# The first of eight feed-forward blocks computed with seven half-sized products, and 320 bytes less of small tiles

## The chip, the cores and the metric

The kernel runs on one core of a Trainium2 chip, in one launch. The metric is device time in microseconds (us): the median over runs of the same program on the chip. TensorE (PE) does the matmuls, VectorE (DVE) and ScalarE (ACT) the elementwise work, GpSimd (POOL) and SyncE (SP) here mostly issue DMAs.

## The reference

One layer of a diffusion backbone for 512 tokens of 2048 features, all in fp32: differential attention and a convolution module, an output projection, a layer norm, and a feed-forward part (FFN) of 8192 inner features with a second layer norm. What the change touches is the end:

```
x  = layer_norm(alpha * x + g1 * y, ln1_g, ln1_b)
h2 = layer_norm(x) * (1 + sc2) + sh2
x  = layer_norm(alpha * x + g2 * (square(relu(h2 @ w_ff1 + b_ff1)) @ w_ff2 + b_ff2), ln2_g, ln2_b)
```

`g2`, `sc2` and `sh2` come from the conditioning vector.

## The kernel before

**Products.** Every fp32 product is three matmuls (`mm3`, L118 to L121): each operand is split into a high part, a rounded copy made by ScalarE (L105), and a low part, the difference made by VectorE (L106). In the names `wh` and `wl` are the halves of a weight tile `w` of 128 x 1024, `h2h` and `h2l` those of the normed input, `fh` and `fl` those of the squared relu. Each weight tile is loaded on SP's queue, copied on ScalarE and subtracted on VectorE before TensorE can use it. `turn["w"]` is the list of pools that the split weights take their tiles from in turn.

**The FFN** goes in eight blocks of 1024 inner features, q = 0 to 7. A block first makes the inner features, eight products n of 128 features with two weight tiles each (tile `f`), then multiplies them with its part of `w_ff2`. There are two ways for the second product:

- `down` (tile `d`): 4 column groups c, 4 pairs of inner features j; 384 matmuls of 512 columns, and the result is multiplied by `g2` and added to the residual `res` at once (`add_gated`). Blocks 0 and 7 use it.
- `down_s` (tile `p`): the 2 x 2 block product of a column half with seven instead of eight half-sized products, 336 matmuls. It needs sums and differences of the inner features (`u1`, `u2`, made on VectorE from a pair of features, tiles `ft` and `fz`) and of weight tiles (L1177). Its sums go to DRAM tensors `accd` on POOL's queue, accumulating from the second block on. Blocks 1 to 6 use it; `ahead` prepares the weights four steps early.

**Block 0** is done in two halves of 256 tokens, because the first layer norm is still running on the second half: `side` is a list of generators whose steps (the projection's end, `ln1_a`, `ln1_b`) are put between the products. The first half goes n = 0 to 7, the second 7, 0 to 6 with the weights of n = 7 kept. Then `gate2` loads `g2`, and `down(0, c, ...)` runs with `bias2` between its weight tiles: eight times a row of `b_ff2` is loaded, multiplied by `g2` (L1091) and added to the residual (L1092). Half of each residual is stored to the DRAM tensors `x1d` on SP's queue after every second c. Block 7 reads `x1d` and `accd` back in `restore` (L1277 to L1279) under its `hidden`, adds its own product, and does the second layer norm.

The order within an engine's queue is not the program's: a scheduler reorders what the functions issue, by its own estimates, before the program is built.

**Where tiles lie.** In each partition the pools lie one behind the other. `const`, `upool` (function `unit`), `rpool`, `wpool` and `tpool` come first, then `small`. `small` begins at a multiple of 512 bytes (185,344) and each of its tiles takes a multiple of 32 bytes. It holds 2880 bytes, which is 5 x 512 + 320, so every pool opened after it, `xw` and `st` among them, begins 320 bytes past a multiple of 512 (188,224), and their large tiles with it. `Pair` gives the weights of blocks 1 to 6 in turn with `wpool`: its `wh` is a tile of `st`, its `wl` one of `upool`.

```
    class Pair:
        def tile(self, shape, dt, tag=None, name=None):
            return unit(name, shape, dt) if tag == "wl" else st.tile(list(shape), dt, tag="H", name=name, bufs=2)

    turn["w"] = [wpool, Pair()]
```

Of the kernel before, what the change touches and what calls it, by code (L numbers as in the profile page):

```python
# [63 lines left out]
def dit_block(ctx, tc, A, out):  # L64
# [1021 lines left out]

    def bias2():
        for i in range(2):
            for t in range(4):
                b = row(5, i, f"bf{t}_{i}")  # L1090
                V.tensor_tensor(b, b, g2[i], op=ALU.mult)  # L1091
                V.tensor_tensor(res[t][i], res[t][i], b, op=ALU.add)  # L1092
                yield

    hid = [None] * 4
# [41 lines left out]
    def hidden_s(n):  # L1137
# [13 lines left out]
        if n % 2:  # L1151
            i = n % 8 // 2
            z = tmp(f"fz{n}", (P, 4, 256))
            V.tensor_tensor(z[:, 0], t[:, 3], t[:, 1], op=ALU.subtract)
            V.tensor_tensor(t[:, 1], t[:, 0], t[:, 1], op=ALU.subtract)
            V.scalar_tensor_tensor(z[:, 1], z[:, 0], -1.0, t[:, 0], op0=ALU.mult, op1=ALU.subtract)
            V.scalar_tensor_tensor(z[:, 2], z[:, 1], -1.0, t[:, 2], op0=ALU.mult, op1=ALU.subtract)
            split(u1[i][0], u1[i][1], t)
            split(u2[0][:, i], u2[1][:, i], z[:, 0:3])
# [284 lines left out]
```

## Time and profile before

| | |
|---|---|
| median of 3 runs | 2401.72 us (2399.5 to 2401.82) |
| profiled execution, its own time | 2405.81 us |
| its span on the core | 2404.0 us |
| mean granted TensorE clock | 0.995 |
| TensorE busy | 2346.1 us, 98% |
| VectorE busy | 1614.9 us, 67% |
| ScalarE busy | 884.0 us, 37% |
| POOL busy | 129.1 us, 5% |

The profiled execution is 4.1 us above the median, and its span is 1.8 us shorter than its time. Times in the trace count from the start of the span. A matmul's row shows a duration that overlaps with the next ones, so the pace is read from the starts. The stages of the FFN, by the first matmul of each: block 0's first half from 1016.65, its second half from 1077.00, `down(0)` from 1124.83, block 1 from 1216.08, block 7 from 2216.01, its `down` from 2304.05.

### The profile page before, as it was taken

How to read it: one execution, taken by the hardware profiler on the slowest of the kernel's cores; microseconds unless marked ns; L12 is line 12 of the kernel's file. 1: busy time of each engine (PE TensorE's matmuls, PEld its weight loads, DVE VectorE, ACT ScalarE, POOL GpSimd, SP SyncE). 2: the span in 40 equal slices, each digit the busy share in tenths (PEclk: the TensorE clock that was granted, in tenths of full speed). 3: DMA queues.
4: the chain of work that ended last, by engine and by line, in shares of the span. 5: the costliest groups of instructions: out<-in, count | busy, mean ns of one | idle time of the engine just before them, and what ended most of it. 6: DMA issues, size and time to landing. Idle time of an engine off the chain costs nothing.

```text
span 2404.0 us, 29326 instructions
## 1 busy us (share of the span) xinstructions
PE 2346.1 (98%) x11476; PEld 1866.2 (78%) x11476; DVE 1614.9 (67%) x2136; ACT 884.0 (37%) x1205; POOL 129.1 (5%) x196
## 2 busy tenths in 40 slices
PE   6999999999999999989999999999999999999998
PEld 4777767777677888889787888888888888888886
DVE  5656999942758777767536846747658558467577
ACT  5223411122535666464223333333334333333322
POOL 0000000000011210000000100100101101002000
PEclk9999999999999999999999999999999999999999
DMA  8665466876877645236542442743534615627652
GB/s 336 246 219 197 164 215 214 289 271 244 293 223 209 164 115 175 88 121 207 173 144 76 159 164 71 165 142 97 141 114 106 192 54 125 192 69 155 214 191 105
DMA packets 126298, 410.87 MB, mean 171 GB/s; under 512 B 15048, under 2 KB 21576, under 8 KB 126160
## 3 DMA queue, kind: packets, MB, share of 16 engines
q1 hardware_dynamic: 107728, 360.76, 43.7%
q0 software_dynamic: 18432, 48.25, 10.0%
q8 instruction: 90, 1.47, 0.3%
q14 instruction: 48, 0.39, 0.0%
HBM read 359.65 MB, written 49.30 MB: 170 GB/s over the span
## 4 chain that ended last, share of the span: by engine, by line
PE 89%; DVE 4%; DMA 3%; ACT 2%; issue 1%; SPq 0%; POOL 0%; DVEq 0%; ACTq 0%
PE f L119 9%; PE f L121 9%; PE f L120 9%; PE p L120 6%; PE p L119 6%; PE p L121 6%; PE gb L219 2%; PE u L119 2%; PE u L120 2%; PE u L121 2%; PE o L580 2%; PE v L119 2%; PE d L121 2%; PE d L120 2%; PE v L120 2%; PE v L121 2%
## 5 line engine op out<-in xcount | busy, mean ns | idle before, releaser
L106 DVE TENSOR_TENSOR wl<-w,wh 128x1024 fp32r<-128x1024 f32 x334 | 404.1, 1221 | 392.1 <-ACT wh L105 391.9
L105 ACT ACTIVATE wh<-w 128x1024 fp32r<-128x1024 f32 x334 | 351.3, 1059 | 742.4 <-PE f L120 274.0
L121 PE MATMUL f<-h2h,wl 128*128 128x512 f32 (+1 forms) x1152 | 425.9, 370 | 3.7 <-DVE wl L106 3.7
L119 PE MATMUL f<-h2h,wh 128*128 128x512 f32 (+1 forms) x1152 | 426.2, 370 | 0.1
L120 PE MATMUL f<-h2l,wh 128*128 128x512 f32 (+1 forms) x1152 | 423.3, 368 | 0.0
L121 PEld LDWEIGHTS f<-h2h,wl 128*128 128x128 f32 x1152 | 218.0, 189 | 44.5 <-DVE wl L106 5.4
L120 PEld LDWEIGHTS f<-h2l,wh 128*128 128x128 f32 x1152 | 218.0, 189 | 38.1
L119 PEld LDWEIGHTS f<-h2h,wh 128*128 128x128 f32 x1152 | 218.2, 190 | 37.2 <-ACT wh L105 0.3
L119 PE MATMUL p<-wh,u1h 128*128 128x512 f32 x384 | 151.5, 395 | 0.0
L120 PE MATMUL p<-wl,u1h 128*128 128x512 f32 x384 | 150.8, 393 | 0.0
L121 PE MATMUL p<-wh,u1l 128*128 128x512 f32 x384 | 149.9, 393 | 0.0
L342 DVE TENSOR_TENSOR ua<-ua,u 128x1024 f32<-128x1024 f32 x64 | 78.0, 1220 | 67.6 <-PE u L121 67.2
L1177 DVE TENSOR_TENSOR w<-w,w 128x1024 f32<-128x1024 f32 x96 | 115.9, 1218 | 0.8
L120 PE MATMUL p<-wl,u2h 128*128 128x512 f32 x288 | 113.7, 395 | 1.3 <-DVE wl L106 1.3
L121 PE MATMUL p<-wh,u2l 128*128 128x512 f32 x288 | 112.9, 392 | 0.0
L119 PE MATMUL p<-wh,u2h 128*128 128x512 f32 x288 | 112.8, 392 | 0.0
L119 PE MATMUL u<-hh,wh 128*128 128x512 f32 x256 | 102.7, 403 | 1.9 <-ACT hh L105 1.9
L120 PE MATMUL u<-hl,wh 128*128 128x512 f32 x256 | 101.9, 398 | 0.0
L121 PE MATMUL u<-hh,wl 128*128 128x512 f32 x256 | 101.1, 395 | 0.0
L282 DVE SCALAR_TENSOR_TENSOR cv<-cv,wdw 128x497 f32<-128x497 f32 (+14 forms) x120 | 89.0, 742 | 3.1
L119 PEld LDWEIGHTS p<-wh,u1h 128*128 128x128 f32 x384 | 72.0, 188 | 17.9 <-ACT u1h L105 1.5
L121 PEld LDWEIGHTS p<-wh,u1l 128*128 128x128 f32 x384 | 71.7, 188 | 17.4 <-DVE u1l L106 1.5
(301 smaller groups left out, 4460.3 us busy)
## 6 DMA issues: line engine op xcount, KB each, us to landing
w<-in_wff_dram SPq DMA_DIRECT2D x174, 512.0 KB, 5.0
wb<-in_wada_dram SPq DMA_DIRECT2D x128, 512.0 KB, 5.7
w<-in_wff2s_dram SPq DMA_DIRECT2D x96, 512.0 KB, 6.2
wa<-in_wada_dram SPq DMA_DIRECT2D x64, 512.0 KB, 6.1
wu<-in_wu_dram SPq DMA_DIRECT2D x32, 512.0 KB, 7.8
k<-kd POOLq DMA_DIRECT2D x64, 192.0 KB, 5.5
accd<-g POOLq DMA_DIRECT2D x48, 256.0 KB, 8.1
accd<-ev POOLq DMA_DIRECT2D x48, 256.0 KB, 5.4
```

The lines of the kernel that those rows point to most:

```text
L105: S.activation(hi, src, AF.Copy)
L106: V.tensor_tensor(lo, src, hi.bitcast(F32), op=ALU.subtract)
L119: T.matmul(ps, lhsT=ah, rhs=bh, start=first, stop=False)
L120: T.matmul(ps, lhsT=ah, rhs=bl, start=False, stop=False)
L121: T.matmul(ps, lhsT=al, rhs=bh, start=False, stop=last)
L219: T.matmul(gps[32 * g:32 * g + 32, 0:n], lhsT=cstat[:, kt, :], rhs=r[:, s * n:(s + 1) * n], start=kt < 4, stop=kt >= 12)
L282: V.scalar_tensor_tensor(dst[:, a:b], src[:, a + d:b + d], wdw[:, j, k:k + 1], dst[:, a:b], op0=ALU.mult, op1=ALU.add)
L342: V.tensor_tensor(uacc[j], uacc[j], ps, op=ALU.add)
L580: T.matmul(ops[:, qt * P:(qt + 1) * P], lhsT=es[1][:, kk * P:(kk + 1) * P], rhs=vh[:, kk, :], start=kk == 0, stop=kk == 5)
L1177: V.tensor_tensor(d, a, b, op=ALU.add)
```

## The change

Four things change together.

- Block 0 uses `down_s` too. A new `hidden_h` computes a product for one half of the tokens and writes the squared relu into one of four tiles `fts` that are kept over both halves; `combine`, the old body of `hidden_s`, runs on such a tile when both features of a pair have their second half. The second half of block 0's `hidden` now comes after the tiles of the first part are closed (`ff.close()`), with weights in `wpool` and `Pair` in turn. The layout of `w_ff2` gives `wff2s` seven blocks and `wff2` one.
- The residual is stored to `x1d` at the end of `ln1_a`, eight stores of 512 KB, on POOL's queue instead of SP's. Block 0's sums are the first to go to `accd`.
- `bias2` and the `gate2` ahead of it go. In block 7 `restore` loads two rows of `b_ff2`, multiplies them by `g2`, and adds them to the eight residual tiles: ten more VectorE operations of 128 x 1024.
- In `small` the filler grows from 8 to 24 floats, and the tiles `mv1`, `rs1`, `l2s`, `l2m` of four token groups and the four tiles `z` give way to four tiles of 16 floats. 64 bytes come, 640 go to 256: 2560 bytes are left, 5 x 512, and every later pool begins at a multiple of 512 bytes (187,904, which is 367 x 512).

```diff
-    small.tile([P, 8], F32, tag="fill", name="fill", bufs=1)
+    small.tile([P, 24], F32, tag="fill", name="fill", bufs=1)
...
-        def sm_(n, w):
-            return small.tile([P, w], F32, tag=f"{n}{g}", name=f"{n}{g}", bufs=1)
-
-        mv, rs, sm, mean = sm_("mv1", 2), sm_("rs1", 1), sm_("l2s", 4), sm_("l2m", 2)
+        sm_ = small.tile([P, 16], F32, tag=f"q{g}", name=f"q{g}", bufs=1)
+        mv, rs, sm, mean = sm_[:, 0:2], sm_[:, 2:3], sm_[:, 4:8], sm_[:, 8:10]
...
+        for i in range(2):
+            nc.gpsimd.dma_start(x1d[g][:, i * 1024:(i + 1) * 1024], us[i])
...
+    fts = [unit(f"ft0_{i}", (P, 4, 256)) for i in range(4)]
+
+    def hidden_h(n, half, keep=False):
+        ps = bk(f"f{n}_{half}")[:, 0:256]
+        sl = slice(256 * half, 256 * half + 256)
...
+        tv = fts[n // 2][:, 2 * (n % 2) + half, :]
+        S.activation(tv, ps, AF.Relu, bias=bff1[:, n:n + 1])
+        V.tensor_tensor(tv, tv, tv, op=ALU.mult)
...
-    turn["w"] = [wpool, xw, wpool]
-    for n in [7, *range(7)]:
-        hidden(n, (1,), hid)
-    turn["w"] = [wpool, wpool, xw]
-    gate2()
-    side.gs = [bias2()]
-    for c in range(4):
-        down(0, c, 0, 4, hid, 2)
-        if c % 2:
-            for t in range(4):
-                nc.sync.dma_start(x1d[t][:, (c // 2) * 1024:(c // 2) * 1024 + 1024], res[t][c // 2])
     ff.close()
...
+    def combine(i, t):
+        z = tmp(f"fz{i}", (P, 4, 256))
+        V.tensor_tensor(z[:, 0], t[:, 3], t[:, 1], op=ALU.subtract)
+        V.tensor_tensor(t[:, 1], t[:, 0], t[:, 1], op=ALU.subtract)
+        V.scalar_tensor_tensor(z[:, 1], z[:, 0], -1.0, t[:, 0], op0=ALU.mult, op1=ALU.subtract)
+        V.scalar_tensor_tensor(z[:, 2], z[:, 1], -1.0, t[:, 2], op0=ALU.mult, op1=ALU.subtract)
+        split(u1[i][0], u1[i][1], t)
+        split(u2[0][:, i], u2[1][:, i], z[:, 0:3])
...
-        if q == 1:
+        if q == 0:
             nc.gpsimd.dma_start(d, e)
...
-    for q in range(1, 7):
-        for n in range(8 * q, 8 * q + 8):
-            hidden_s(n)
...
+    for q in range(7):
+        if q == 0:
+            for m, n in enumerate([7, *range(7)]):
+                hidden_h(n, 1)
+                if n in (1, 3, 5, 6):
+                    combine(n // 2, fts[n // 2])
+                if m == 6:
+                    load_raw(q, 0, 1)
...
         load_raw(q, 0, 0)
+        if q == 0:
+            load_raw(q, 0, 2)
         load_raw(q, 0, 3)
...
     def restore():
+        b2 = [unit(f"b2_{i}") for i in range(2)]
         for i in range(2):
+            nc.sync.dma_start(b2[i], A["rows"][5:6, i * 1024:(i + 1) * 1024].partition_broadcast(P).rearrange("p a d -> p (a d)"))
+            V.tensor_tensor(b2[i], b2[i], g2[i], op=ALU.mult)
...
+                V.tensor_tensor(u, u, b2[i], op=ALU.add)
                 V.tensor_tensor(u, u, a, op=ALU.add)
...
-                sm = small.tile([P, 8], F32, tag=f"z{t}", name=f"zs{t}", bufs=1)
+                sm = small.tile([P, 16], F32, tag=f"q{t}", name=f"zs{t}", bufs=1)
```

The place that the prediction speaks of most is where block 0's second half of `hidden` ends and its second product begins. On VectorE before, the last weight splits `w_5_1`, `w_6_0` and `w_6_1` (inner product n, weight tile j) alternate with single squares, `fl` splits and the operations of `gate2` (L1084) and `bias2` (L1091, L1092):

```order
1104 L106 TENSOR_TENSOR wl<-w_5_1_9321,wh 128x1024
1105 L1084 TENSOR_TENSOR g_0_9422<-g_0_9422,bg_0_9424 128x1024
1106 L106 TENSOR_TENSOR wl<-w_6_0_9357,wh 128x1024
1107 L1056 TENSOR_TENSOR ft_9285<-ft_9285 128x256
...
1109 L106 TENSOR_TENSOR fl_8623<-ft_9285,fh_8622 128x256
1110 L106 TENSOR_TENSOR wl<-w_6_1_9387,wh 128x1024
1111 L1091 TENSOR_TENSOR bf_0_9442<-bf_0_9442,g_0_9422 128x1024
1112 L106 TENSOR_TENSOR wl<-w_0_0_0_9436,wh 128x1024
1113 L1056 TENSOR_TENSOR ft_9351<-ft_9351 128x256
1114 L1092 TENSOR_TENSOR r_0_5356<-r_0_5356,bf_0_9442 128x1024
```

After the change VectorE has here the chain of the third combine (`u1l_8884`, `u2l`), the split of `w_6_1`, two weight additions (L1173), and the chain of the fourth combine (tile `ft_3`). `w_0_0_0_0` and `w_0_0_0_1` are the weights of the second product's first steps:

```order
1111 L106 TENSOR_TENSOR u1l_8884<-ft_2_8264,u1h_8883 128x1024
1112 L106 TENSOR_TENSOR u2l<-fz_9336,u2h 128x768
1113 L106 TENSOR_TENSOR wl<-w_6_1_9380,wh 128x1024
1114 L1173 TENSOR_TENSOR w_0_0_0_0_9421<-w_0_0_0_0_9421,w_0_0_1_0_9345 128x1024
...
1116 L1099 TENSOR_TENSOR ft_3_8265<-ft_3_8265 128x256
1117 L1150 TENSOR_TENSOR fz_9412<-ft_3_8265 128x256
...
1121 L106 TENSOR_TENSOR u1l_8886<-ft_3_8265,u1h_8885 128x1024
1122 L106 TENSOR_TENSOR u2l<-fz_9412,u2h 128x768
1123 L106 TENSOR_TENSOR wl<-w_0_0_0_0_9421,wh 128x1024
1124 L106 TENSOR_TENSOR wl<-w_0_0_0_1_9423,wh 128x1024
```

What moved: the split of `w_6_1`, which stood behind a single `fl`, now stands behind a whole chain, and the splits of the first summed weights stand behind the next one.

On TensorE before, the last product of `hidden` (`f_1_9356`) ends whole and the second product (`d`) follows. After the change the last product (`f_1_9349`, n = 6) is cut: 26 of its matmuls stand ahead of 18 of the second product, that use the first three combines (u1h, u1l with the numbers 8879 to 8884), and 22 behind them:

```order
4765 L120 MATMUL f_1_9349<-h2l_8182,wh 128x256
4766 L119 MATMUL p_0_0_0_9451<-wh,u1h_8879 128x512
...
4783 L121 MATMUL p_0_0_1_9452<-wh,u1l_8884 128x512
4784 L121 MATMUL f_1_9349<-h2h_8181,wl 128x256
...
4805 L121 MATMUL f_1_9349<-h2h_8239,wl 128x256
4806 L119 MATMUL p_0_1_0_9470<-wh,u2h 128x512
4807 L119 MATMUL p_0_1_1_9471<-wh,u2h 128x512
4808 L119 MATMUL p_0_0_0_9451<-wh,u1h_8885 128x512
...
4812 L121 MATMUL p_0_0_0_9451<-wh,u1l_8886 128x512
...
4814 L120 MATMUL p_0_1_0_9470<-wl,u2h 128x512
```

What moved: behind the last matmul of `hidden` only two matmuls stand ahead of the ones that need the fourth combine (`u1h_8885`, `u1l_8886`). Further up, the products n = 2 to 5 are cut and interleaved in the same way.

## Rows read from the trace of the kernel before

**Rows 1.** The page: busy time by engine, and the last-ended chain by engine.

```profile
PE 2346.1 (98%) x11476; PEld 1866.2 (78%) x11476; DVE 1614.9 (67%) x2136; ACT 884.0 (37%) x1205; POOL 129.1 (5%) x196
PE 89%; DVE 4%; DMA 3%; ACT 2%; issue 1%; SPq 0%; POOL 0%; DVEq 0%; ACTq 0%
```

**Rows 2.** Stretches of block 0, blocks 1 to 6, one `down_s`, block 7: length, then busy time and count by engine, clock, DMA share, GB/s.

```profile
1016.65:1077.00 60.35, 51.94 (x406) 50.92 (x405) 43.14 (x72) 35.48 (x57) 0.00 (x0) 0.94 0.35 109
1077.00:1124.83 47.83, 47.72 (x400) 47.51 (x399) 29.95 (x38) 26.17 (x43) 0.00 (x0) 1.00 0.59 193
1124.83:1216.08 91.25, 89.18 (x387) 71.97 (x386) 52.87 (x61) 17.75 (x18) 0.00 (x0) 1.00 0.50 167
1216.08:2216.01 999.93, 998.66 (x4321) 809.62 (x4320) 643.87 (x726) 358.61 (x385) 75.60 (x94) 1.00 0.45 127
1473.02:1551.15 78.13, 78.13 (x338) 62.71 (x336) 63.01 (x71) 32.39 (x34) 11.07 (x14) 1.00 0.54 120
2216.01:2304.05 88.04, 88.04 (x386) 72.11 (x385) 49.46 (x57) 24.96 (x30) 1.74 (x2) 1.00 0.70 221
```

**Rows 3.** Timeline of TensorE, one `hidden_s` product: start, duration, line and tiles.

```profile
1396.99 0.39 PE L119 MATMUL f<-h2h,wh 128*128 128x512 f32 x1
...
1400.84 0.39 PE L121 MATMUL f<-h2h,wl 128*128 128x512 f32 x1
1401.07 0.40 PE L119 MATMUL f<-h2h,wh 128*128 128x512 f32 x1
...
1406.43 0.39 PE L121 MATMUL f<-h2h,wl 128*128 128x512 f32 x1
```

**Rows 4.** Timeline of TensorE, in `down_s` of block 1.

```profile
1324.80 0.39 PE L121 MATMUL p<-wh,u1l 128*128 128x512 f32 x1
...
1326.16 0.39 PE L121 MATMUL p<-wh,u1l 128*128 128x512 f32 x1
1326.39 0.40 PE L119 MATMUL p<-wh,u1h 128*128 128x512 f32 x1
...
1328.95 0.40 PE L121 MATMUL p<-wh,u1l 128*128 128x512 f32 x1
```

**Rows 5.** Timeline of TensorE, the one wait in blocks 1 to 6.

```profile
1312.94 0.50 PE L120 MATMUL p<-wl,u2h 128*128 128x512 f32 x1 [1.27 <-DVE wl L106]
```

**Rows 6.** The page, costliest groups: TensorE on u.

```profile
L119 PE MATMUL u<-hh,wh 128*128 128x512 f32 x256 | 102.7, 403 | 1.9 <-ACT hh L105 1.9
```

**Rows 7.** Groups by line in 1124.83 to 1216.08 (`down(0)`): busy, mean | idle before.

```profile
L120 PE MATMUL d<-wl,fh 128*128 128x512 f32 x128 | 50.4, 394 | 2.1 <-DVE wl L106 2.1
L1092 DVE TENSOR_TENSOR r<-r,bf 128x1024 f32<-128x1024 f32 x8 | 9.5, 1217 | 0.0
```

**Rows 8.** Timeline of VectorE, one pair's chain in block 1.

```profile
1239.82 0.69 DVE L1150 TENSOR_TENSOR ft<-ft 128x512 f32<-128x512 f32 x1 [4.94 <-ACT ft L1149]
1240.55 0.42 DVE L1154 TENSOR_TENSOR fz<-ft 128x256 f32<-128x256 f32 x1
...
1242.56 1.23 DVE L106 TENSOR_TENSOR u1l<-ft,u1h 128x1024 fp32r<-128x1024 f32 x1 [0.33 <-ACT u1h L105]
1243.70 0.95 DVE L106 TENSOR_TENSOR u2l<-fz,u2h 128x768 fp32r<-128x768 f32 x1
```

**Rows 9.** Groups by line in 1016.65 to 1077 (first half of block 0).

```profile
L121 PE MATMUL f<-h2h,wl 128*128 128x256 f32 x123 | 36.3, 295 | 3.7 <-DVE wl L106 3.7
L105 ACT ACTIVATE wh<-w 128x1024 fp32r<-128x1024 f32 x13 | 13.4, 1056 | 11.0 <-PE f L120 9.4 <-issue 1.4 <-DMA w<-in_wff_dram 0.2
L1055 ACT ACTIVATE ft<-f,pk 128x256 f32<-128x256 f32 x7 | 3.2, 466 | 6.5 <-PE h2p L949 2.9 <-DVE r L745 2.0 <-PE f L121 1.6
```

**Rows 10.** The page, DMA issues: KB each, us from issue to landing.

```profile
accd<-g POOLq DMA_DIRECT2D x48, 256.0 KB, 8.1
```

**Rows 11.** Groups by line in 2216.01 to 2304.05 (block 7's `hidden`), VectorE.

```profile
L1279 DVE TENSOR_TENSOR s<-s,ac 128x1024 f32<-128x1024 f32 x8 | 9.5, 1221 | 0.6 <-DMA s<-x1d 0.6
L1277 DVE TENSOR_TENSOR ac<-ac,g 128x512 f32<-128x512 f32 x8 | 5.5, 691 | 8.2 <-DMA ac<-accd 8.2
```

More of the change, by code (lines that the diff above doesn't have):

```diff
@@ L1040, in dit_block, with hidden @@
     side.gs = [wout_end(1, ps), ln1_a(2), ln1_a(3), ln1_b(1)]
-    def hidden(n, halves, hid, keep=False):
-        sl = slice(256 * halves[0], 256 * halves[-1] + 256)
-        ps = bk(f"f{n}_{halves[0]}")[:, sl]
+    def hidden(n, hid):
+        sl = slice(0, 512)
+        ps = bk(f"f{n}")
         for j in range(2):
-            wh, wl = w1.pop((n, j)) if (n, j) in w1 else weights(A["wff1"][n, j], f"w1_{n}_{j}")
-            if keep:
-                w1[n, j] = wh, wl
+            wh, wl = weights(A["wff1"][n, j], f"w1_{n}_{j}")
             for k in range(8):
@@ L1060, in hidden, with down @@
         split(hi[:, n % 2, sl], lo[:, n % 2, sl], tv)
-    def down(q, c, j0, j1, hid, n=0):
+    def down(q, c, j0, j1, hid):
         ps = [bk(f"d{q}_{c}_{t}") for t in range(4)]
         for j in range(j0, j1):
-            wh, wl = weights(A["wff2"][q // 7, c, j], f"w2_{q}_{c}_{j}")
-            side.step(n)
+            wh, wl = weights(A["wff2"][0, c, j], f"w2_{q}_{c}_{j}")
             hi, lo = hid[j]
@@ L1085, in gate2 @@
             g2.append(u)
-    def bias2():
-        for i in range(2):
-            for t in range(4):
[L1090 to L1095, printed above, removed]
+    fts = [unit(f"ft0_{i}", (P, 4, 256)) for i in range(4)]
+    def hidden_h(n, half, keep=False):
+        ps = bk(f"f{n}_{half}")[:, 0:256]
+        sl = slice(256 * half, 256 * half + 256)
+        for j in range(2):
+            wh, wl = w1.pop((n, j)) if (n, j) in w1 else weights(A["wff1"][n, j], f"w1_{n}_{j}")
+            if keep:
+                w1[n, j] = wh, wl
+            for k in range(8):
+                kt = 8 * j + k
+                bh, bl = h2k(kt, sl)
+                mm3(ps, wh[:, k * P:(k + 1) * P], wl[:, k * P:(k + 1) * P], bh, bl, kt == 0, kt == KT - 1)
+        tv = fts[n // 2][:, 2 * (n % 2) + half, :]
+        S.activation(tv, ps, AF.Relu, bias=bff1[:, n:n + 1])
+        V.tensor_tensor(tv, tv, tv, op=ALU.mult)
     turn["w"] = [wpool, wpool, xw]
@@ L1099, in dit_block @@
             turn["w"] = [wpool, wpool, xw, wpool, wpool, xw, wpool, Units()]
-        hidden(n, (0,), hid, n == 7)
+        hidden_h(n, 0, n == 7)
         side.step(4)
     side.flush()
-    turn["w"] = [wpool, xw, wpool]
-    for n in [7, *range(7)]:
-        hidden(n, (1,), hid)
-    turn["w"] = [wpool, wpool, xw]
-    gate2()
-    side.gs = [bias2()]
-    for c in range(4):
-        down(0, c, 0, 4, hid, 2)
-        if c % 2:
-            for t in range(4):
-                nc.sync.dma_start(x1d[t][:, (c // 2) * 1024:(c // 2) * 1024 + 1024], res[t][c // 2])
     ff.close()
@@ L1151, in hidden_s @@
         if n % 2:
[L1152 to L1159, printed above, removed]
+            combine(n % 8 // 2, t)
+    def combine(i, t):
[6 more added lines that the diff above has]
+        split(u2[0][:, i], u2[1][:, i], z[:, 0:3])
     raws, ws = {}, {}
@@ L1164, in load_raw @@
         for jj in range(2):
-            src = A["wff2s"][q - 1, cp, kind, jj]
+            src = A["wff2s"][q, cp, kind, jj]
             if kind in (1, 2):
@@ L1253, in dit_block @@
     LEAD = 4
-    for q in range(1, 7):
-        for n in range(8 * q, 8 * q + 8):
-            hidden_s(n)
-            if n % 8 == 4:
-                load_raw(q, 0, 1)
-                load_raw(q, 0, 2)
+    for q in range(7):
[6 more added lines that the diff above has]
+                    load_raw(q, 0, 1)
+        else:
+            for n in range(8 * q, 8 * q + 8):
+                hidden_s(n)
+                if n % 8 == 4:
+                    load_raw(q, 0, 1)
+                    load_raw(q, 0, 2)
         load_raw(q, 0, 0)
+        if q == 0:
+            load_raw(q, 0, 2)
         load_raw(q, 0, 3)
@@ L1285, in dit_block @@
         for n in range(8 * q, 8 * q + 8):
-            hidden(n, (0, 1), hid)
+            hidden(n, hid)
             if n % 8 == 0:
@@ L1298, in dit_block @@
                 for j in (2, 3):
-                    r = load(A["wff2"][q // 7, c, j], f"w2_{q}_{c}_{j}")
+                    r = load(A["wff2"][0, c, j], f"w2_{q}_{c}_{j}")
                     for s in range(2):
@@ L1384, in _layout @@
     w2 = w_ff2.reshape(8, 4, 2, P, 4, 512)
-    o["wff2"] = c(w2[[0, 7]].transpose(0, 4, 1, 3, 2, 5)).reshape(2, 4, 4, P, 1024)
-    w2 = w2[1:7].reshape(6, 2, 2, 2, P, 2, 2, 512)
+    o["wff2"] = c(w2[7:].transpose(0, 4, 1, 3, 2, 5)).reshape(1, 4, 4, P, 1024)
+    w2 = w2[:7].reshape(7, 2, 2, 2, P, 2, 2, 512)
     w2 = np.stack([w2[:, :, :, a, :, :, b] for a, b in ((0, 0), (0, 1), (1, 1), (1, 0))])
-    o["wff2s"] = c(w2.transpose(1, 5, 0, 2, 4, 3, 6)).reshape(6, 2, 4, 2, P, 1024)
+    o["wff2s"] = c(w2.transpose(1, 5, 0, 2, 4, 3, 6)).reshape(7, 2, 4, 2, P, 1024)
     o["rows"] = c(np.stack([b_ada[2 * D:3 * D], b_ada[5 * D:6 * D], inp["b_out"][0], inp["ln1_g"][0], inp["ln1_b"][0],
```

## The prediction

> **What bounds the kernel now.** I read the page first: TensorE is busy for 98% of the span and holds 89% of the chain that ended last [rows 1]. So only two things can shorten the run: fewer or quicker matmuls, and the few places where TensorE stands still. I then cut the span into stages [rows 2]. From 1216.08 to 2216.01 (blocks 1 to 6) TensorE is busy for 998.66 of 999.93 us, so nothing but the pace of its matmuls counts there. VectorE is busy for 643.87 us of it, so it has room. The first block is different: in its first half TensorE works 51.94 of 60.35 us, and in its second product 89.18 of 91.25.
>
> Next I took the pace, since the stages are longer than their counts. A matmul of 512 columns starts every 226.5 ns in one half of a `hidden_s` product (17 intervals from 1396.99 to 1400.84) and every 233.0 ns in the other (23 intervals from 1401.07 to 1406.43) [rows 3]. Shape, line and moving operand are the same; only the weights' tiles differ. The first half has its weights in `wpool`, the second in `Pair`, whose high part is a tile of the pool `st`. By the sizes told above, `wpool` lies on a multiple of 512 bytes and `st` 320 past one. In `down_s` the same two rotations appear as moving operands, and again there are two paces: 226.67 ns (6 intervals from 1324.80 to 1326.16) and 232.7 (11 from 1326.39 to 1328.95) [rows 4]. I take 226.67 as the bare pace and 6.5 ns as what a slow tile adds. That it is the address and not something else in `Pair` is a reading of these rows, not shown by them.
>
> **The change, part by part.** Sums are against the profiled execution, 2405.81 us, which is 4.1 above the median of 2401.72; I subtract that at the end.
>
> *1. The pace in blocks 1 to 7.* The small pool gets 320 bytes shorter, so every pool opened after it moves to a multiple of 512. Blocks 1 to 6 hold 6 x (384 + 336) = 4320 matmuls, at 226.67 ns 979.2 us, against 999.93 [rows 2]: 20.7 us over, with a single wait of 1.27 us in it [rows 5]. Block 7's `hidden` takes 88.04 against 87.04: 1.0 more. At most 21.7 us come back, at least none, if the pace has another cause. I take 20, near the upper end, because the quick halves run at exactly the bare pace, and leave 1.7 for the wait and the changes between tiles. The moving tiles of `Pair` will start at an odd multiple of 512, which no row shows. **-20** (0 to -21.7).
>
> *2. The pace before the first block.* Weights of u, v, q and the output projection partly lie in the shifted pools too. u alone has 3 x 256 matmuls [rows 6]; a third of them at 6.5 ns is 1.7 us, all of u 5. **-2** (0 to -5).
>
> *3. The second product of block 0.* `down(0)` has 384 matmuls and takes 91.25 us [rows 2]; `down_s(0)` has 336, at 226.67 ns 76.2 us. This is 15.1 less: 48 x 0.2267 = 10.9 for the matmuls, 2.1 for the waits for `wl` [rows 7], which stand where bias2 puts eight additions of 1.22 us and as many products into VectorE's queue, and the rest pace. Against it stands the new entrance. `combine` may run only when both features of a pair are there; in blocks 1 to 6 a pair takes two products of 48 matmuls with 512 columns, here it takes two with 256, half as long (47.83 us for eight [rows 2], so 12 for a pair). Its chain on VectorE is the square, four subtractions of 0.42, u1l 1.23 and u2l 0.95, from 1239.82 to 1244.6 [rows 8]. For three of the four the order puts parts of the next products between, so TensorE has other work. For the last the order has VectorE do the split of `w_6_1` after the third combine, then two additions, then the fourth chain and only then the two `wl` of the second step. I follow TensorE through this with the same durations: a wait for `wl` of `w_6_1` of about 1.6 us; then relu 0.47, square 0.42, two subtractions 0.85 and ScalarE's copy 1.06 [rows 9], less 0.45 for two matmuls in between, 2.4; u1l after the four matmuls on u1h 0.3; u2l and `wl` behind it 1.6; half a `wl`, 0.8, for the rest. The sum is 6.7 us. Bounds: 0, as at the entrance of blocks 2 to 6, where TensorE has no gap (78.13 us busy of 78.13), and 12, if the fourth chain (5) and four `wl` (5) and both additions (2.4) end one after the other in the open. **-15.1 + 6.7 = -8.4** (-15.1 to -3).
>
> *4. First half of block 0, LN1 and stores.* Eight `fh`/`fl` splits leave, each 0.42 us on two engines, as a subtraction of that size [rows 8]. TensorE waits there for a `wl` for 3.7 us [rows 9], behind LN1's operations on VectorE; a shorter queue can bring that in, a new order can add as much again. **-1** (-3 to +3). The eight stores of x1d go from SP to POOL's queue, which is idle here [rows 2], right after LN1. Who waits for them: the units they read are taken over by u1l of the second combine and by weight tiles, so VectorE's queue, with the `wl` behind it, waits if a store is late. They are issued some 30 us ahead; an accumulating store on POOL takes 8.1 us to land [rows 10]. Cost 0.
>
> *5. `restore` in block 7.* Ten operations of 1.22 us come [rows 11], 12.2 us of VectorE, and two loads on SP. VectorE is busy for 49.46 of 88.04 us there, of which it waited 8.2 for accd [rows 11]; 62 of 88 leaves the cover intact. If it goes, what is late is one `wl` by 1.22. **+0.5** (0 to +2).
>
> Sum: -20 - 2 - 8.4 - 1 + 0.5 = -30.9; 2405.8 - 30.9 = 2374.9 profiled, and 4.1 less, 2370.8, is what I expect of the median: **2371 us**.
>
> The rows of one shape show a pace that goes with the tile. The Trainium skill, page "SBUF — State Buffer", section "Specifications (TRN2)", gives cachelines of 16 bytes, and its "Operand start alignment" asks only for a multiple of the element's size and says that this is about legality and that nothing was timed. 320 is 20 such lines, so by that page terms 1 and 2 would be nothing and the sum 2393. I go by the rows.
>
> **Rivals.**
> *A. The pace does not follow the address* (it is `Pair`'s two pools, or the change of tile). Terms 1 and 2 fall away: -8.4 - 1 + 0.5 = -8.9, so 2393. For it: one and the same pool is always the slow one in the rows. Against it: two roles, stationary and moving, show the same 6.5 ns. Chance 0.09. The cachelines cited above would make it this one.
>
> *B. Half the pace comes back*, in `hidden_s` and not in `down_s`, whose moving tiles lie at an odd multiple of 512, or since VectorE gets late there as TensorE gets quicker (63.01 busy of 78.13 now, of 76.2 then [rows 2]). `down_s` is about 1.5 to 2 us over its bare pace in each of six blocks, about 11 in all: 2382. Chance 0.15.
>
> *C. The end on the other side: the combine chain on VectorE's in-order queue holds up block 0.* Its place is the second half of `hidden`. Each of the four chains puts 3.9 us (four subtractions, u1l, u2l) ahead of the next `wl`, and each product lasts only 6 us; if the interleaved products don't cover it, four times 3.9 and 0.4 for ScalarE are 17 us, and with the entrance at 12 the stalls are 29. That alone takes away -15.1 and leaves -8 with the pace's gain. It is slower than before only if the pace gives less than 29 - 15.1 - 0.5 = about 13 us too; with none of it 2402 + 14 = 2416. For it: VectorE stands in one queue for splits, squares and combines. Against it: VectorE's work per pair is four `wl` (4.9), two squares and the chain (4.7), under 10 of 12 us. Chance 0.03.
>
> **How the numbers follow.** Forecast 0.73 (2359 to 2381), B 0.15 (2382), A 0.09 (2393), C 0.03. The range goes from 2359, where the pace comes back whole, u gives 5, the entrance costs 3 and the first half gains 3 (-21.7 - 5 - 12 - 3 = -41.7, of 2401.7), to 2390, which takes in B with an entrance at its upper bound (2382 + 5) and 3 from the first half; A lies outside. A measurement of this kernel can tell about 0.2%, 4.8 us. Faster by more: the forecast, B and most of A, 0.94; within: the rest of A and a mild C, 0.04; slower: the rest of C, 0.02.
>
> **What would show it.** Right: in blocks 1 to 6 a stage of `hidden_s` takes 87.0 to 87.3 us and one of `down_s` 76.2 to 76.6, and the `Pair` half starts a matmul every 226.7 ns. The second product of block 0 lasts 80 to 84, with one cluster of waits for `u1h`, `u1l` and `wl` at its entrance and none later. Block 7's first product stays at 87 to 88 with VectorE at about 62. The forecast is wrong if the `Pair` halves still take 233 ns (A), if `down_s` stays at 77.7 (B), or if waits for `wl` follow each combine in the second half of block 0's `hidden`, making it more than 52 us (C).

## The result, and the profile after

The median of the changed kernel is **2375.93 us** (2372.51 to 2379.19, five runs), that of the kernel before 2401.72 in five runs too. The ratio is 0.9895, 95% interval 0.9881 to 0.9908: faster by 25.8 us. The forecast was 2371, the range 2359 to 2390.

The profiled execution took 2373.51 us, 2.4 below its median, where the one before was 4.1 above its own. So 6.5 of the 32.3 us between the two traces are scatter. Most of that lies in the attention: from the last matmul of q to the first of y the trace before has 218.7 us, this one 214.6, and the other twelve traces below have 211.1 to 216.6, whichever version they are of.

The page, the counterpart of [rows 1]:

```profile
PE 2315.1 (98%) x11428; PEld 1854.5 (78%) x11428; DVE 1641.2 (69%) x2160; ACT 900.3 (38%) x1213; POOL 147.1 (6%) x220
PE 80%; DVE 7%; issue 6%; DMA 5%; ACT 2%; POOL 0%; SPq 0%; DVEq 0%; ACTq 0%; POOLq 0%
```

TensorE's busy time fell by 31 us and VectorE's rose by 26. The chain runs through TensorE for 80% instead of 89%; issue has 6% instead of 1, VectorE 7 instead of 4, DMA 5 instead of 3.

The stages, as in [rows 2]: length, busy time and count of PE, PEld, DVE, ACT, POOL, clock, DMA share, GB/s. They are block 0's `hidden` with the entrance of its second product, the rest of that product, blocks 1 to 6, one `down_s` (block 2), then block 7's `hidden`, `down` and last part with the tail:

```profile
1008.93:1118.49 109.56, 104.78 (x822) 102.22 (x821) 77.31 (x113) 63.78 (x92) 2.13 (x4) 0.97 0.47 159
1118.49:1195.54 77.05, 74.14 (x320) 60.22 (x319) 69.49 (x77) 33.73 (x35) 7.60 (x14) 0.98 0.39 139
1195.54:2180.81 985.27, 984.77 (x4322) 808.60 (x4320) 638.85 (x719) 356.37 (x383) 81.24 (x96) 1.00 0.48 127
1446.57:1523.58 77.01, 76.97 (x337) 62.72 (x336) 62.79 (x71) 32.38 (x34) 10.84 (x14) 1.00 0.54 121
2180.81:2268.16 87.35, 87.34 (x386) 72.00 (x385) 53.97 (x62) 24.62 (x29) 2.19 (x3) 1.00 0.67 213
2268.16:2313.36 45.20, 43.86 (x194) 35.96 (x193) 40.47 (x52) 12.79 (x13) 0.00 (x0) 1.00 0.63 212
2313.36:2371.50 58.14, 44.54 (x193) 35.69 (x191) 46.32 (x86) 14.93 (x24) 0.00 (x0) 0.93 0.26 98
```

Against the stages before, by the first matmuls of each: block 0 186.6 instead of 199.4 us; blocks 1 to 6 985.3 instead of 999.9; block 7's `hidden` 87.35 instead of 88.04, but its `down` 45.20 instead of 44.31 and its last part up to the last matmul 46.7 instead of 44.4.

The pace, one product of block 2, the counterpart of [rows 3] (timeline of TensorE):

```profile
1381.29 0.39 PE L119 MATMUL f<-h2h,wh 128*128 128x512 f32 x1
...
1386.50 0.39 PE L121 MATMUL f<-h2h,wl 128*128 128x512 f32 x1
1386.73 0.39 PE L119 MATMUL f<-h2h,wh 128*128 128x512 f32 x1
...
1391.94 0.39 PE L121 MATMUL f<-h2h,wl 128*128 128x512 f32 x1
```

The weights of the first half are in `wpool`, those of the second, from 1386.73, in `Pair`. 23 intervals in either half are 5.21 us, 226.5 ns each. The slow half is gone, and a stage of `hidden_s` takes 87.04 us, which is 384 x 226.67 ns to the digit.

The entrance of block 0's second product (TensorE's rows that waited):

```profile
1112.25 0.74 PE L121 MATMUL p<-wh,u1l 128*128 128x512 f32 x2 [0.28 <-DVE u1l L106]
1114.26 0.38 PE L121 MATMUL f<-h2h,wl 128*128 128x256 f32 x1 [1.27 <-DVE wl L106]
1121.68 0.79 PE L119 MATMUL p<-wh,u1h 128*128 128x512 f32 x1 [2.57 <-ACT u1h L105]
1124.95 0.50 PE L120 MATMUL p<-wl,u2h 128*128 128x512 f32 x1 [0.34 <-DVE wl L106]
```

The last matmul of `hidden` is followed by 2.57 us for `u1h` of the fourth combine; ahead of it TensorE waits 1.27 for the `wl` of `w_6_1`, behind it 0.34 for a summed `wl`. Start to start and over the pace, the 13.36 us from 1111.59 to 1124.95 hold 8.2 us too much, where the price was 6.7. About 5.5 of it are these waits. The rest is the clock: behind each of the two long waits the granted clock falls to 0.50, the lower of its two levels (1.2 GHz). The matmuls of `hidden` from 1114.62 to 1117.82 start every 0.213 us, where those from 1103.84 to 1108.04 started every 0.120; with their neighbours that is 1.6 us. Five of the second product, from 1121.68, start 0.43 to 0.59 us apart instead of 0.227, which is 1.2. The two slow stretches, in the columns of the stages above:

```profile
1114.62:1117.82 3.20, 3.20 (x17) 3.20 (x16) 1.85 (x2) 1.06 (x1) 0.00 (x0) 0.50 0.80 257
1121.68:1123.98 2.30, 2.30 (x5) 1.82 (x6) 2.30 (x3) 0.69 (x1) 0.00 (x0) 0.50 0.00 0
```

The waits of 0.28, 1.27 and 2.57 us come out within 0.01 us in e2, e3, e5 and e6 below, but the clock does not fall at the same places: in e3 the stretch from the wait for `wl` to the one for `u1h` takes 5.9 us instead of 7.4.

Block 7, VectorE at the beginning of `down`, and TensorE's waits in `down` and the last part (us in total, times, longest):

```profile
2271.18 1.22 DVE L1288 TENSOR_TENSOR s<-s,b 128x1024 f32<-128x1024 f32 x1
2272.61 1.23 DVE L1288 TENSOR_TENSOR s<-s,b 128x1024 f32<-128x1024 f32 x1 [0.21 <-DMA s<-x1d]
2273.75 2.35 DVE L1289 TENSOR_TENSOR s<-s,ac 128x1024 f32<-128x1024 f32 x2
2276.03 0.68 DVE L1054 TENSOR_TENSOR ft<-ft 128x512 f32<-128x512 f32 x1
2276.63 1.21 DVE L1288 TENSOR_TENSOR s<-s,b 128x1024 f32<-128x1024 f32 x1
2277.76 0.68 DVE L106 TENSOR_TENSOR fl<-ft,fh 128x512 fp32r<-128x512 f32 x1
2278.36 1.21 DVE L1289 TENSOR_TENSOR s<-s,ac 128x1024 f32<-128x1024 f32 x1
2279.50 2.35 DVE L106 TENSOR_TENSOR wl<-w,wh 128x1024 fp32r<-128x1024 f32 x2
```

```profile
PE z L120 <- DVE w2l L106: 1.6, 1, 1.6
PE d L120 <- DVE wl L106: 1.3, 1, 1.3
PE z L119 <- ACT w2h L105: 1.0, 2, 0.7
```

All of this is after 2268.16, when `down` has begun: three of the eight bias additions (L1288), one of which waits 0.21 us for a load of x1d, and three additions of the sums (L1289). Before the change all eight of the latter lay within `hidden` [rows 11]. So VectorE is busy for 53.97 us in block 7's `hidden`, and not for the 62 that were forecast. From 2273.75 on VectorE has no gap, and the two `wl` at 2279.50, that `down` needs, stand behind all of it. TensorE then waits for `wl` and `w2l`.

### The profile page after: what moved, and what is told of

It is laid out like the page before. It is cut to its first block, busy times and chain, and to the rows that moved or that the text cites. A ratio compares the mean times of both kernels' runs of the same rounds, so it can differ in the third digit from the quotient of the medians.

```text
span 2371.5 us, 29292 instructions
## 1 busy us (share of the span) xinstructions
PE 2315.1 (98%) x11428; PEld 1854.5 (78%) x11428; DVE 1641.2 (69%) x2160; ACT 900.3 (38%) x1213; POOL 147.1 (6%) x220
## 4 chain that ended last, share of the span: by engine, by line
PE 80%; DVE 7%; issue 6%; DMA 5%; ACT 2%; POOL 0%; SPq 0%; DVEq 0%; ACTq 0%; POOLq 0%
PE f L121 9%; PE f L119 9%; PE f L120 9%; PE p L120 6%; PE p L121 6%; PE p L119 6%; PE u L119 3%; PE u L120 2%; PE u L121 2%; PE gb L219 2%; PE v L119 2%; PE v L121 2%; PE v L120 2%; DVE wl L106 2%; PE o L580 2%
## 5 line engine op out<-in xcount | busy, mean ns | idle before, releaser
L106 DVE TENSOR_TENSOR wl<-w,wh 128x1024 fp32r<-128x1024 f32 x346 | 418.5, 1221 | 376.4 <-ACT wh L105 376.3
L105 ACT ACTIVATE wh<-w 128x1024 fp32r<-128x1024 f32 x346 | 364.1, 1059 | 705.8 <-PE f L120 258.6
L119 PE MATMUL p<-wh,u1h 128*128 128x512 f32 x448 | 175.7, 392 | 2.6 <-ACT u1h L105 2.6
L120 PE MATMUL p<-wl,u1h 128*128 128x512 f32 x448 | 174.8, 390 | 0.0
L121 PE MATMUL p<-wh,u1l 128*128 128x512 f32 x448 | 173.9, 391 | 0.3 <-DVE u1l L106 0.3
L1173 DVE TENSOR_TENSOR w<-w,w 128x1024 f32<-128x1024 f32 x112 | 135.0, 1218 | 0.8
L120 PE MATMUL p<-wl,u2h 128*128 128x512 f32 x336 | 132.6, 395 | 0.8 <-DVE wl L106 0.3
L121 PE MATMUL p<-wh,u2l 128*128 128x512 f32 x336 | 131.0, 390 | 0.0
L119 PE MATMUL p<-wh,u2h 128*128 128x512 f32 x336 | 130.6, 390 | 0.0
L121 PEld LDWEIGHTS p<-wh,u1l 128*128 128x128 f32 x448 | 83.8, 188 | 19.1 <-DVE u1l L106 2.0
L120 PEld LDWEIGHTS p<-wl,u1h 128*128 128x128 f32 x448 | 84.4, 188 | 17.3
```

The source lines that it names most:

```text
L105: S.activation(hi, src, AF.Copy)
L106: V.tensor_tensor(lo, src, hi.bitcast(F32), op=ALU.subtract)
L119: T.matmul(ps, lhsT=ah, rhs=bh, start=first, stop=False)
L120: T.matmul(ps, lhsT=ah, rhs=bl, start=False, stop=False)
L121: T.matmul(ps, lhsT=al, rhs=bh, start=False, stop=last)
L1173: V.tensor_tensor(d, a, b, op=ALU.add)
```

## The experiments

**1 and 2. The two halves of the change apart.** The kernel before with the small tiles of the change, and the changed kernel with the 320 bytes put back.

```diff
 e1, on the kernel before
-    small.tile([P, 8], F32, tag="fill", name="fill", bufs=1)
+    small.tile([P, 24], F32, tag="fill", name="fill", bufs=1)
...
+        sm_ = small.tile([P, 16], F32, tag=f"q{g}", name=f"q{g}", bufs=1)
+        mv, rs, sm, mean = sm_[:, 0:2], sm_[:, 2:3], sm_[:, 4:8], sm_[:, 8:10]
...
+                sm = small.tile([P, 16], F32, tag=f"q{t}", name=f"zs{t}", bufs=1)
 e2, on the changed kernel
-    small.tile([P, 24], F32, tag="fill", name="fill", bufs=1)
+    small.tile([P, 104], F32, tag="fill", name="fill", bufs=1)
```

> The kernel before with the change's small tiles alone, so that every later pool begins at a multiple of 512 bytes; the order of every queue is that of before. If the pace follows the address: each hidden_s stage 87.0 us instead of 88.5, each down_s about 76.2 to 77, blocks 1 to 6 985 to 987 us instead of 999.9, down(0) 89 to 90, and 3 to 8 us before block 0; in all 21 to 27 us off, 2375 to 2381. If the pace goes with the pool and not with its address (rival A): 2400 to 2403, the Pair halves still at 233 ns.

> The changed kernel with a filler of 104 instead of 24 floats, so that the later pools begin 320 bytes past a multiple of 512 again, as before; same order. If the pace follows the address: hidden_s 88.5, down_s 77.7 to 78.5, 18 to 25 us over the changed kernel, 2394 to 2400. If not: 2373 to 2379. What then still separates it from the kernel before is the worth of block 0's seven products with their price in block 7: I expect 2 to 8 us in favour of the change.

e1: 2382.56 us, ratio 0.9928 (0.9911 to 0.9944). e2: 2391.68, ratio 0.9962 (0.9947 to 0.9977). Blocks 1 to 6 and one `hidden_s` of block 2, e1 and then e2:

```profile
1209.05:2194.27 985.22, 983.67 (x4322) 809.30 (x4320) 642.09 (x725) 358.48 (x385) 74.07 (x93) 1.00 0.46 129
1375.10:1462.14 87.04, 87.04 (x385) 72.11 (x384) 41.68 (x48) 26.08 (x30) 1.08 (x2) 1.00 0.37 124
```

```profile
1198.66:2195.78 997.12, 997.11 (x4321) 810.62 (x4320) 639.07 (x719) 356.47 (x383) 81.15 (x96) 1.00 0.47 126
1364.76:1453.26 88.50, 88.50 (x386) 72.18 (x384) 43.21 (x49) 26.55 (x31) 1.73 (x2) 1.00 0.43 135
```

Each fell on the side of the address theory, though e1 gave 18 us and not 21 or more, and e2 lies 2 under its band and 9.0 below the kernel before, where 8 at most was expected. `hidden_s` is 87.04 or 88.5 with the address, in either program. What e1's stages from block 0 on gained (1.7 in block 0, 14.7 in blocks 1 to 6, 2.0 in block 7) is 18.4 and thus all of the 18.1, so nothing of it has to come from ahead of block 0. Alone the address is worth 18.1 us and block 0 with its price in block 7 9.0; together they gave 25.8. By the stages, blocks 1 to 6 differ by 14.7 between e1 and before and by 11.9 between the changed kernel and e2. `down_s` is where the address pays less than it could: in blocks 2 to 6 it takes 77.6 to 78.0 us in e2, 77.0 to 77.5 in the changed kernel, 76.5 to 77.2 in e1.

**3, 4 and 8. How far off is off?** The changed kernel with 256, 64 and 128 more bytes in the filler.

```diff
-    small.tile([P, 24], F32, tag="fill", name="fill", bufs=1)
+    small.tile([P, 88], F32, tag="fill", name="fill", bufs=1)     e3; 40 in e4, 56 in e8
```

> The changed kernel with 256 more bytes in the filler: later pools at 256 past a multiple of 512. If what counts is a multiple of 64, 128 or 256 bytes (320 is 5 x 64, and no multiple of 128), the Pair halves start a matmul every 226.7 ns and the time is that of the changed kernel, 2372 to 2379. If it takes a multiple of 512: 233 ns, 2394 to 2400.

> The changed kernel with 64 more bytes in the filler: later pools at 64 past a multiple of 512. If 64 bytes are enough, 320 would have been too, so by the address theory this is slow: 233 ns in the Pair halves, 2394 to 2400. By rival A it is 2372 to 2379.

> The changed kernel with 128 more bytes in the filler: later pools at 128 past a multiple of 512. 64 and 320 were slow, 256 and 0 quick. If a multiple of 128 is enough: 226.7 ns in the Pair halves, hidden_s 87.0; if it takes 256: 233 ns, hidden_s 88.5, and 14 to 18 us more than the changed kernel.

One run each: 2373.62, 2390.29 (4 under its band) and 2391.61 us. `hidden_s` of block 2 in e3, e4 and e8:

```profile
1360.66:1447.70 87.04, 87.04 (x385) 72.10 (x384) 43.20 (x49) 26.75 (x31) 1.74 (x2) 1.00 0.44 138
```

```profile
1364.07:1452.56 88.49, 88.49 (x385) 72.12 (x384) 43.11 (x49) 26.70 (x31) 1.73 (x2) 1.00 0.43 134
```

```profile
1366.49:1454.96 88.47, 88.47 (x386) 72.14 (x384) 43.24 (x49) 27.27 (x31) 1.73 (x2) 1.00 0.43 135
```

Of the offsets tried, 0 and 256 are quick, and 64, 128 and 320 cost the same 1.4 to 1.5 us in a stage. So a multiple of 256 bytes is enough and one of 128 is not, and the loss doesn't grow with the distance. Offsets below 64 and 192 were not tried.

**9 and 10. Which operand?** Padding inside the pool `st` shifts only one kind of tile by 128 bytes.

```diff
 e9: Pair's wh alone
     u2 = [st.tile([P, 4, 3, 256], F32R, name=f"u2{z}") for z in "hl"]
+    st.tile([P, 32], F32, name="pad")
 e10: u2 alone
+    st.tile([P, 32], F32, name="pad")
     u2 = [st.tile([P, 4, 3, 256], F32R, name=f"u2{z}") for z in "hl"]
+    st.tile([P, 32], F32, name="pad2")
```

> The changed kernel with a tile of 128 bytes in the pool st behind u2, so that Pair's wh alone lies at 128 past a multiple of 256; every other tile as in the changed kernel. If the address of the stationary operand is enough: Pair's half of hidden_s at 231 to 234 ns, hidden_s 88.2 to 88.6. If that of the moving operand is enough: Pair's steps of down_s above 227 ns too, down_s 77.3 to 77.8 with few waits for wl. If the pace went with the pool and not with its address, this would be the changed kernel's time, 2372 to 2379; by the address 2385 to 2392.

> The changed kernel with 128 bytes ahead of u2 and 128 behind it in the pool st: u2, the stationary operand of three of the seven products, lies at 128 past a multiple of 256, Pair's wh at 256 past one of 512. hidden_s has no shifted operand: 87.0. If a shifted stationary operand is enough, the matmuls of down_s on u2 start every 231 to 234 ns, and down_s takes 77 to 78 us without waits; if not, 226.7 ns and 76.4 to 77.5.

e9: 2385.65 us in one run, e10: 2375.21 in one. `hidden_s` and `down_s` of block 2, e9 and then e10:

```profile
1361.07:1449.54 88.47, 88.47 (x386) 72.12 (x385) 43.14 (x49) 26.88 (x31) 1.73 (x2) 1.00 0.44 135
1449.54:1526.91 77.37, 77.37 (x338) 62.82 (x336) 62.96 (x71) 32.37 (x34) 10.98 (x14) 1.00 0.54 122
```

```profile
1360.02:1447.06 87.04, 87.04 (x386) 72.07 (x384) 43.06 (x49) 26.15 (x30) 1.74 (x2) 1.00 0.43 137
1447.06:1524.53 77.47, 77.47 (x338) 62.92 (x337) 62.92 (x71) 32.38 (x34) 10.95 (x14) 1.00 0.53 121
```

In `hidden_s` `wh` is the stationary operand, and it alone brings back the whole loss of 1.43 us. In e10 nothing of `hidden_s` is shifted, and it stays at 87.04, while all six `down_s` take 77.3 to 77.5. Its timeline of TensorE in `down_s`, first steps on `u2`, then on `u1`:

```profile
1457.60 0.39 PE L119 MATMUL p<-wh,u2h 128*128 128x512 f32 x1
...
1463.65 0.40 PE L121 MATMUL p<-wh,u2l 128*128 128x512 f32 x1
...
1466.43 0.39 PE L121 MATMUL p<-wh,u1l 128*128 128x512 f32 x1
...
1469.15 0.40 PE L121 MATMUL p<-wh,u1l 128*128 128x512 f32 x1
```

26 intervals on `u2` from 1457.60 give 232.7 ns, 12 on `u1` from 1466.43 give 226.7. A shifted stationary operand is enough. For the moving one e9's `down_s` speaks, at 77.25 to 78.0. Its length holds late `wl` too, but one stretch of it has none (no interval over 236 ns), and there the 144 intervals take 229.4 ns each; in the changed kernel 151 intervals from 1458.65 on take 226.7. Only `Pair`'s `wh` is shifted there, as moving operand, so that is enough too, at a smaller price over steps of which half use it:

```profile
1466.26:1499.30 33.04, 33.04 (x145) 27.03 (x144) 28.30 (x32) 11.10 (x11) 6.82 (x8) 1.00 0.81 177
```

**5 and 6. What the bias costs in block 7.** e5 leaves `b_ff2` out of `restore`. e6 adds it early, in DRAM, where POOL's queue has room.

```diff
 both
-        b2 = [unit(f"b2_{i}") for i in range(2)]
...
-                V.tensor_tensor(u, u, b2[i], op=ALU.add)
 e6
+    def bias2():
+        for i in range(2):
+            b = unit(f"b2_{i}")
+            nc.sync.dma_start(b, A["rows"][5:6, i * 1024:(i + 1) * 1024].partition_broadcast(P).rearrange("p a d -> p (a d)"))
+            V.tensor_scalar(b[:, 512:], b[:, 512:], -1.0, None, op0=ALU.mult)
+            for t in range(4):
+                nc.gpsimd.dma_start(accd[t][:, i * 1024:(i + 1) * 1024], b, accum_op=ALU.add)
...
                 hidden_s(n)
+                if n == 8:
+                    bias2()
```

> The changed kernel without b_ff2 in restore: the two loads, the two products and the eight additions of 128 x 1024 are left out, and with them the second product's bias. If these additions on VectorE are what delays the wl of block 7's down and the w2l of its last part: hidden 87.1, down 43.6, z 44.2 instead of 87.35, 45.20, 46.71; 4 to 5 us less than the changed kernel, about 2369 to 2374. If the waits come from the quicker TensorE alone: the three stages as in the changed kernel, 2372 to 2379.

> The changed kernel with b_ff2 added to the sums in DRAM at the start of block 1: two rows are loaded, one half of each negated on VectorE (2 x 0.69 us), and eight accumulating stores of 512 KB go on POOL's queue; restore as before the change. If restore's additions cost 4.5 us and block 1 has room: 4 to 5 us less than the changed kernel, ratio to the kernel before 0.986 to 0.989. If the stores delay block 1's own or the units: waits in block 1, and nothing gained.

e5: 2365.73 us in one run, 3 under its band, with the three stages as expected. e6: 2366.54, ratio 0.9853 (0.9836 to 0.9869), a little more than expected. Blocks 1 to 6 and the three stages of block 7 in e6:

```profile
1195.49:2178.78 983.29, 983.09 (x4322) 809.40 (x4320) 639.13 (x721) 356.66 (x383) 87.42 (x103) 1.00 0.50 133
2178.78:2265.82 87.04, 87.04 (x386) 72.08 (x384) 50.87 (x58) 24.30 (x29) 2.91 (x4) 1.00 0.71 224
2265.82:2309.34 43.52, 43.52 (x194) 36.04 (x192) 36.67 (x51) 13.78 (x14) 0.00 (x0) 1.00 0.60 190
2309.34:2364.80 55.46, 43.98 (x193) 35.78 (x191) 43.64 (x81) 13.87 (x23) 0.00 (x0) 0.93 0.24 92
```

Block 7 up to its last matmul is 179.3 us in the changed kernel and 174.6 in both e5 and e6. The waits are gone, so they came from the additions. That is 4.7 us in the traces; e6's median is 9.4 below that of the changed kernel. Blocks 1 to 6 give 2 more, and the rest is within the two intervals.

**7 and 11. The entrance.** The preparation of the first summed weights is written ahead of the last product of `hidden`; e7 on the changed kernel, e11 on e6.

```diff
+                if m == 7:
+                    ahead(q, 0)
+                    ahead(q, 1)
                 hidden_h(n, 1)
...
-                if m == 6:
+                if m == 5:
                     load_raw(q, 0, 1)
+                    load_raw(q, 0, 0)
```

> The changed kernel with the first two weight preparations of block 0's second product written ahead of the last product of hidden, and their loads one step earlier; PE's order then has 43 instead of 20 matmuls of the second product ahead of the end of hidden. If the 6.5 us of waits at the entrance come from the summed weights' wl standing behind the last combine: 2 to 4 us of waits there instead of 6.5, block 0 from its first to its last matmul 183 to 185 instead of 186.6. If it is the latency of the last combine alone: 5 to 7 us of waits.

> b_ff2 added early to the sums in DRAM (2366.5 by itself) and the two weight preparations ahead of the last product of hidden (1.2 us off block 0 in the last look). If the two add up: 2364 to 2367, ratio to the kernel before 0.9845 to 0.986. If the new order of the entrance only moves its waits: 2365 to 2369.

e7: 2373.77 us in one run, block 0 185.4 instead of 186.6. e11: 2371.22, ratio 0.9878 (0.9859 to 0.9897), not better than e6 and rather worse. Some of TensorE's waits in e7:

```profile
1098.84 0.39 PE L121 MATMUL f<-h2h,wl 128*128 128x256 f32 x1 [0.76 <-DVE wl L106]
1108.54 0.39 PE L119 MATMUL f<-h2h,wh 128*128 128x256 f32 x1 [0.78 <-ACT wh L105]
1123.38 0.50 PE L119 MATMUL p<-wh,u1h 128*128 128x512 f32 x1 [1.39 <-ACT u1h L105]
1126.64 0.50 PE L120 MATMUL p<-wl,u2h 128*128 128x512 f32 x1 [1.27 <-DVE wl L106]
```

The wait for `u1h` is 1.39 instead of 2.57, the one for `w_6_1` is gone, and others came: these two inside `hidden`, with a third of 0.24, and one of 1.27 for the `wl` behind. The new order mostly moved the waits. Nor is the 1.2 us off block 0 shown to be its gain: in e3, e5 and e6, whose edits lie elsewhere, it takes 187.1, 185.2 and 186.5 us. One difference is the clock, which stays at 1.00 from 1108.54 to 1126.64 in e7 and was 0.80 from 1108.16 to 1124.95 in the changed kernel. The second expectation of e11 named a mere move, and its time was missed upwards by 2 us. What the 4.7 us between e11 and e6 are stays open. It isn't block 0, 186.2 us in e11 and 186.5 in e6; of the 2.7 us between their two traces 2.4 lie ahead of block 0, where the kernels don't differ.

**12. Is VectorE late in `down_s`?** e6, with the additions of the seventh product on POOL.

```diff
         elif p == 6:
-            add(v, x, v)
+            nc.gpsimd.tensor_tensor(v, x, v, op=ALU.add)
```

> b_ff2 added early, and one of the four kinds of weight additions of down_s (the sum x + v of the seventh product, four of sixteen additions a block) on POOL instead of VectorE. If down_s stays 0.3 to 1.4 us over its bare 76.2 because VectorE's queue is late: 76.3 to 76.6 in each block, 1 to 4 us less than with b_ff2 early alone, 2363 to 2366. If POOL's addition takes longer than the four steps that it has, or VectorE is slowed while POOL works: waits for the wl of the seventh product, 2367 to 2380.

2365.18 us, ratio 0.9846 (0.9828 to 0.9864): the lowest of all, and against e6 no difference that the runs can tell. The trace tells one. Blocks 1 to 6, then the addition on POOL and the `wl` on VectorE in the first `down_s`:

```profile
1191.55:2172.37 980.82, 980.82 (x4321) 809.76 (x4320) 643.22 (x698) 357.59 (x383) 145.75 (x128) 1.00 0.48 134
```

```profile
L1182 POOL TENSOR_TENSOR w<-w,w 128x1024 f32<-128x1024 f32 x4 | 9.9, 2475 | 114.9 <-DMA w<-in_wff2s_dram 97.3 <-issue 17.6
```

```profile
L106 DVE TENSOR_TENSOR wl<-w,wh 128x1024 fp32r<-128x1024 f32 x28 | 37.1, 1335 | 12.9 <-ACT wh L105 12.7
```

Six `down_s` take 76.41 to 76.45 us each, against 76.45 to 77.25 in e6, and blocks 1 to 6 are at 980.8, 1.6 over the bare 979.2. So VectorE's queue was what kept `down_s` above its pace. VectorE is not less busy than before; that what counts is which of its operations are late is argued, see the last section.

## Why the prediction was right

Step by step, in us; the measured sizes are from the traces.

| step | forecast | measured |
|---|---|---|
| 1. pace in blocks 1 to 7 | -20 (0 to -21.7) | -14.7 in blocks 1 to 6 (11.9 by e2), -2.0 in block 7 by e1 |
| 2. pace before block 0 | -2 (0 to -5) | -0.4 in the output projection, the rest inside the scatter |
| 3. second product of block 0 | -15.1 + 6.7 = -8.4 | 83.2 for 91.25: -8.1; 7.0 over the bare 76.2 |
| 4. first part of block 0 | -1 (-3 to +3) | -4.7, the 1.6 us of slow clock in its last product included |
| 5. `restore` | +0.5 (0 to +2) | +4.7 |

The 83.2 us are the time of the second product's matmuls, from 1108.16 to 1114.26 and from 1118.49 to 1195.54; what `hidden` has between them counts to step 4. The measured steps sum to -25.2, the medians differ by 25.8. The lower end of the range does not add up: 2401.7 - 41.7 is 2360.0, not 2359.

**The reading of the two paces was right,** and the runs have made it more than a reading: the same program is quick or slow with 64, 128 or 320 bytes of padding (e2, e4, e8), and padding one tile slows its stage alone (e9, e10). Rival A is out. The rule weighed there, lines of 16 bytes by the Trainium skill's page "SBUF — State Buffer", section "Specifications (TRN2)", does not explain it: 64, 128 and 320 are whole numbers of such lines and cost 1.4 to 1.5 us in each `hidden_s`.

**Step 1 failed in size, for `down_s`.** `hidden_s` gave all of it, 6 x 1.45 and 0.7 in block 1. `down_s` gave 0.1 to 1.1 in blocks 2 to 6 instead of 1.5 to 2, and stays 6.1 us over its bare pace in the six blocks: rival B, which had 11, came in by half. The reason is the second half of rival B, not the first: odd multiples of 512 don't matter (e12 keeps them and takes 76.4), but VectorE gets late as TensorE gets quicker. e12 shows it: with four of VectorE's sixteen additions a block on POOL, 19.1 us come back in blocks 1 to 6. I had the cover of VectorE in `down_s` on the page, 63 busy of 76, and took the share for the answer.

**Step 3 was right in its two main waits, and in its sum partly by luck.** The chain of rows on VectorE and ScalarE priced the wait for `u1h`, 2.4 forecast and 2.57 found, and for `w_6_1`, 1.6 and 1.27. The last two terms, 1.6 and 0.8 for u2l and the `wl` behind, came to 0.34. The sum held because the clock, which the forecast didn't price, took 1.2 us here and 1.6 more in the last product of `hidden`. No wait followed the first two combines but 0.8 at 1087.24, so rival C did not come.

**Step 4 was too small.** Before, TensorE waited twice for `xn` (1.28 and 3.76 us, start to start) and 3.5 for a `wl`; now, in the same stretch, for a `wl` alone:

```profile
L121 PE MATMUL f<-h2h,wl 128*128 128x256 f32 x121 | 35.1, 290 | 2.6 <-DVE wl L106 2.6
```

The clock has a part in it: its granted mean was 0.94 in the first half before [rows 2]. That the splits which left both queues let the layer norm end earlier is argued from the rows, and no run takes it apart; in e6 and e7 a wait of 0.8 for `xn` is back.

**Step 5 failed.** "62 of 88 leaves the cover intact" is a mean over the stage. The additions don't spread over it as they like: three come when it has ended, in a `down` where VectorE has 36.7 of 43.5 us of its own work (e6). e5 and e6 show 4.7 us. Steps 4 and 5 missed in opposite ways and cancelled to 0.5 us, which is luck. Step 1 missed 3.3 and step 2 1.6; that is most of the 5 us by which the median lies above the forecast, inside the range.

## What to carry to other kernels

Look at the pace of long runs of one matmul shape: if a stage has two paces that go with the tile, check where the tiles begin. A few hundred bytes of small tiles ahead of the big pools shifted everything behind them here, and their sum, set by a filler tile, decides the pace of half the weights (e3 against e2). And when an engine off the path gets more work, count the room in the part of the stage where its inputs have arrived and ahead of the next thing that waits in its queue, not in the stage as a whole.

## What the runs showed of the hardware

- fp32 matmuls of 512 columns start every 226.7 ns with tiles on multiples of 256 bytes, and about 6 ns later when the stationary operand begins at 64, 128 or 320 past (e2, e4, e8, e10). After the last shifted tile the old pace holds on: in e10 eleven intervals on `u1` from 1463.89 to 1466.43 still take 231 ns each, with nothing shifted. The same tail follows matmuls that were a little late: in the changed kernel two intervals at 1454.05 take 269 and 336 ns, and nine from 1456.56 to 1458.65 still 232. So a late `wl` costs `down_s` more than its own delay.
- At the entrance of block 0's second product the granted clock fell to 0.50 (1.2 GHz) behind waits of 1.27 and 2.57 us of TensorE, and the matmuls after them took nearly twice as long, 2.8 us in all.
- POOL's addition of 128 x 1024 takes 2.4 to 2.7 us against VectorE's 1.22, and it slows VectorE beside it: the mean `wl` in a `down_s` takes 1335 ns in e12 and 1222 in e6, below. In blocks 1 to 6 of e12 the 23 `wl` that overlap one of POOL's additions take 1.9 to 3.0 us, the 240 others 1.23 at most. So VectorE's busy time in blocks 1 to 6 did not fall (639.1 in e6, 643.2 in e12). That it helped by which operations are late is argued from this.

```profile
L106 DVE TENSOR_TENSOR wl<-w,wh 128x1024 fp32r<-128x1024 f32 x27 | 32.8, 1222 | 13.4 <-ACT wh L105 13.4
```
